# A pair's decays and learning rates, worked out one window earlier

## The chip, the cores and the metric

The kernel runs on one core of a Trainium2 chip. Its time is the device time of one execution in microseconds (us). Before the change, three runs took 1234.54, 1236.76 and 1237.37 us; the median is 1236.76 us. A smaller time is better.

The engines' names are those of the profile: PE multiplies matrices, PEld loads its weights, DVE and ACT work on vectors (ACT also has the tables for tanh, exp and the like), POOL does a few small steps, and SP issues the transfers (DMA) between the large memory and the core's own.

## The reference, cut to what matters

Two layers, each with one mixer. One input projection of the normalised x gives the inputs of two groups of heads; what the change touches is group A, a recurrent mixer that runs over the 256 positions forwards and backwards:

```
h = rms_norm(x, norm_g[l]);  proj = h @ w_in[l]
r, k, v, xw, xa = split(bidir_token_shift(rw_in))
lw = tanh(xw)
for d in (forward, backward):
    decay = exp(-exp(-softplus(-(w0[d] + lw @ decay_up[d])) - 0.5))
    a = sigmoid(a0[d] + xa @ iclr_up[d])          # the learning rates
    kk = k * k_k, normalised within its head
    kd = k * (1 + (a - 1) * k_a)
    S = S * decay - (S kk) (a kk)^T + v kd^T;  y += S r     # position by position
x = x + concat(y_A * silu(g_A), y_B * silu(g_B)) @ w_out[l]
```

Group B is windowed attention. After the second layer comes a last normalisation. decay_up and iclr_up are the low-rank factors (96 rows; with w0 as a further row decay_up has 97) that this document calls du and iu. Group A has 16 heads of 64 channels; the kernel works on pairs of heads, 8 pairs a layer, 128 channels each.

## The kernel before

**The stream of projections.** All large products are cut into output tiles of 128 columns. A tile takes 16 steps, one for each 128 rows of its weights, and a step is three matmuls of 128x256 (L286 to L288), since weights and activations are each split into a high and a low part. The weights come in halves of 8 steps: SP loads `raw` (L208), ACT writes `hi` (L216), DVE writes `lo` (L218). There are three buffers for `raw`, two each for `hi` and `lo`. `Stream.run(n)` emits the next n steps; the function that empties a finished tile (its "evac") is called behind its last step.

**Windows and slots.** A layer starts with two tiles of 16 steps (xw, xa), and then runs in windows of 64 steps, that is four tiles. `window` (L373) cuts a window into 14 slots of four or five steps: slot s begins after step 64*s//14. At the start of each slot it advances the generators that are listed for it, each to its next `yield`, and so puts the mixer's own work between the projections. Window w (0 to 7) projects pair w: k in steps 0 to 15, v to 31, r to 47, the gate gr to 63. From window 8 on the projections are those of the attention. After window 12 the output projection follows with 256 steps, and then the next layer.

**A pair's way through the windows.** Pair p is projected in window p. `scan_p` (L646) prepares it in window p+1, at the slots of STAGE_P. `scan_i` (L724) inverts its chunks in window p+2 and the first two slots after it, and `scan_b` (L874) runs the recurrence in windows p+3 and p+4. So in windows 3 to 7 three or four pairs are in work at once. `scans` (L954) lists the generators with their lag in windows.

`scan_p` has nine stages, at slots 4, 5, 6, 7, 8, 9, 10, 11 and 13:

1. The low-rank products into `pza` (12 matmuls, L636 to L638), ACT's tanh of both (LW for the decay, TH for the learning rate), the square of k (tile `t1`, which the profile calls `t`) and KR.
2. DVE adds 1 to LW and makes two running sums (L672).
3. The head sums `pk` (L642) of the square, ACT's two exponentials PP and IP, DVE's reciprocal KD.
4. to 8. A chain on DVE, which fills MV and BK, and ends with two steps in `km` (tile `lw`).
9. The head sums `pbn` of `km`, and `bv`.

**The low-rank weights.** `ups` (L468) issues the transfers of iu (96 rows, L472) and du (97 rows) into two `g` tiles when the pair's k tile begins. These two buffers are also those of the gate's evacuation (`silu_evac`, L420). `value_evac` (L476) splits them behind the v tile, at step 32: ACT writes iuh and duh (L455), DVE iu and du (L456), each in a single buffer, which the pair before must have read.

**What sets the order.** PE works strictly in the order of the program (`manual_schedule`, L137). For the other engines the framework's planner lays down, when the kernel is built, in which order each engine takes its instructions; among those that it holds to be ready the program's order decides, with a lead for the blocks under `high_priority`. Instructions issued through `PA` (ACT) and `PV` (DVE) keep the program's order among themselves; the splits of iu and du are not among them. At run time each engine takes its list in the given order and waits for whatever is not there yet. SP's queue is such a list too.

Of the kernel before, what the change touches and what calls it, by code (L numbers as in the profile page):

```python
# [15 lines left out]
AF = mybir.ActivationFunctionType  # L16
# [5 lines left out]
T = 256  # L22
# [13 lines left out]
P_NG, P_MU0, P_MU1, P_KK, P_KA, P_RK, P_LG, P_LB, P_A0 = 0, 16, 42, 68, 76, 84, 92, 100, 108  # L36
# [5 lines left out]


SLOTS = 14
STAGE_P = [4, 5, 6, 7, 8, 9, 10, 11, 13]
STAGE_I = (list(range(SLOTS)), [0, 1])
STAGE_B = (list(range(1, 14)), [1, 2, 3, 4])
ATT = [
# [81 lines left out]
def hybrid_trunk_kernel(ctx, tc, xT, wi, wv, wo, par, fing, dup, iup, sink, pos, cst, out):  # L130
# [17 lines left out]
    def wpair(name):  # L148

        return ps_w.tile([128, 2, 512], F32, tag="w", name=name)  # L150

    def wbank(name):
        return wpair(name)[:, 0]

    def st(tag, shape, dt=F32, bufs=1):
        return sp.tile([128, *shape], dt, tag=tag, name=tag, bufs=bufs)
# [76 lines left out]
    PA, PV = InTurn(A), InTurn(V)  # L233
# [167 lines left out]
    def queue_inputs(l):  # L401
        L = layers[l]
        prm = lambda o, j: PR[:, l, o + j : o + j + 1]
        dpm = lambda o, j: DP[:, l, o + j : o + j + 1]

        def inproj(ct, evac, **kw):
            gemm(wi[l, ct], lambda: (L.XH, L.XL), evac, **kw)

        def shift_evac(j, place):
            def evac(pm):  # L410
                dst = place()
                u = st("u", [T], bufs=2)
                V.tensor_tensor(u, pm, L.norm.rb, op=ALU.mult)
                A.activation(dst, u, AF.Identity, scale=dpm(0, j))
                V.scalar_tensor_tensor(dst[:, 1:T], u[:, 0 : T - 1], prm(P_MU0, j), dst[:, 1:T], op0=ALU.mult, op1=ALU.add)
                V.scalar_tensor_tensor(dst[:, 0 : T - 1], u[:, 1:T], prm(P_MU1, j), dst[:, 0 : T - 1], op0=ALU.mult, op1=ALU.add)

            return evac
# [11 lines left out]
        def new(t, name, tag, bufs):  # L430
            def place():
                t[name] = st(tag, [T], bufs=bufs)
                return t[name]

            return place
# [37 lines left out]

            return begin

        def value_evac(p, t):  # L476
            ev = shift_evac(8 + p, new(t, "v", "vg", 8))

            def evac(pm):
                ev(pm)  # L480
                for n, rows in (("iu", RANK), ("du", RANK + 1)):
                    raw = t[n]
                    t[n] = (st(n + "h", [2, 128], F32R), st(n, [2, 128], F32R))
                    split(t[n], raw, rows)

            return evac

        for p, t in enumerate(L.ts):
            inproj(2 + 4 * p, shift_evac(p, new(t, "k", "kr", 4)), begin=ups(p, t))
            inproj(3 + 4 * p, value_evac(p, t))  # L490
            inproj(4 + 4 * p, shift_evac(16 + p, new(t, "r", "kr", 4)))
            inproj(5 + 4 * p, silu_evac(new(t, "gr", "vg", 8)))


# [71 lines left out]
        for n in ("q0", "q1", "q2", "q3", "g0", "q4", "g1", "q5", "g2", "q6", "g3", "q7", "g4", "g5", "g6", "g7"):  # L566
            j = int(n[1])
# [52 lines left out]
    def layer(l):  # L620
# [14 lines left out]
        def low_rank(o, w, x):  # L635
            PE.matmul(o, w[0], x[0], start=True, stop=False)  # L636
            PE.matmul(o, w[0], x[1], start=False, stop=False)
            PE.matmul(o, w[1], x[0], start=False, stop=True)  # L638

        def head_sums(o, x):  # L640
            for r in half:
                PE.matmul(o[r, 0:T], bones[r, r], x[r, 0:T], start=True, stop=True)  # L642

        def scan_p(p, t):  # L646
            K, VV, R, iu, du = t["k"], t["v"], t["r"], t["iu"], t["du"]
            dd = lambda x: x.rearrange("p (d x) -> p d x", d=2)
            two = lambda x: x.unsqueeze(1).to_broadcast([128, 2, T])
            c8 = lambda x: x.rearrange("p (n j) -> p n j", j=64)  # L650

            pza = wpair("pza")
            pz, pa = pza[:, 0], pza[:, 1]
            for d in range(2):
                low_rank(pz[:, d * T : (d + 1) * T], [a[0 : RANK + 1, d, :] for a in du], [a[0 : RANK + 1] for a in L.TW])
            LW = st("lw", [2 * T])
            for d in range(2):
                low_rank(pa[:, d * T : (d + 1) * T], [a[0:RANK, d, :] for a in iu], [a[0:RANK] for a in L.XA])
            PA.activation(LW, pz, AF.Tanh, scale=0.5)
            TH = st("th", [2 * T])  # L660
            for d in range(2):
                PA.activation(TH[:, d * T : (d + 1) * T], pa[:, d * T : (d + 1) * T], AF.Tanh, scale=0.5, bias=dpm(NSH + 16, d * 8 + p))
            sq = st("t1", [T], bufs=3)
            PA.activation(sq, K, AF.Square, scale=prm(P_KK, p))
            KR = st("kkr", [T])
            PA.activation(KR, K, AF.Identity, scale=prm(P_KK, p))
            yield

            PV.tensor_scalar(LW, LW, 1.0, None, op0=ALU.add)
            msk = MSK.rearrange("p c j -> p (c j)")  # L670
            for x in (LW[:, 0:T], LW[:, T : 2 * T][:, ::-1]):
                PV.tensor_tensor_scan(x, msk, x, 0.0, op0=ALU.mult, op1=ALU.add)  # L672
            yield
            pk = wbank("pk")
            head_sums(pk, sq)
            PP = st("pp", [2, NC, 64])
            IP = st("ip", [2, NC, 64])
            PA.activation(PP.rearrange("p d c j -> p (d c j)"), LW, AF.Exp, scale=DECAY_C)
            PA.activation(IP.rearrange("p d c j -> p (d c j)"), LW, AF.Exp, scale=-DECAY_C)
            KD = st("kd", [T])  # L680
            PV.reciprocal(KD, pk[:, 0:T])
            PV.scalar_tensor_tensor(KD, KD, 1e24, KR, op0=ALU.min, op1=ALU.mult)
            yield

            MV = st("mv", [2, NC, 2, 64], bufs=3)
            BK = st("bk", [2, NC, 3, 64])
            km = st("lw", [2 * T])
            kr4 = KR.rearrange("p (c j) -> p c j", j=64)
            PV.scalar_tensor_tensor(MV[:, 0, :, 0, 1:64], PP[:, 0, :, 0:63], -1.0, kr4[:, :, 1:64], op0=ALU.mult, op1=ALU.mult)
            PV.scalar_tensor_tensor(MV[:, 1, :, 0, 0:63], PP[:, 1, :, 1:64], -1.0, kr4[:, :, 0:63], op0=ALU.mult, op1=ALU.mult)  # L690
            PA.activation(MV[:, 0, :, 0, 0:1], kr4[:, :, 0:1], AF.Copy, scale=-1.0)
            PA.activation(MV[:, 1, :, 0, 63:64], kr4[:, :, 63:64], AF.Copy, scale=-1.0)
            PA.activation(km, TH, AF.Identity, scale=dpm(NSH, p), bias=dpm(NSH + 8, p))
            yield
            PV.scalar_tensor_tensor(dd(TH), dd(TH), 1.0, two(KD), op0=ALU.add, op1=ALU.mult)
            BK8 = BK.rearrange("p d c s j -> p (d c) s j")
            IP8 = IP.rearrange("p d c j -> p (d c) j")
            PV.scalar_tensor_tensor(BK8[:, :, 1, :], c8(TH), 0.5, IP8, op0=ALU.mult, op1=ALU.mult)
            yield
            PV.tensor_tensor(dd(km), dd(km), two(K), op=ALU.mult)  # L700
            PV.tensor_tensor(BK8[:, :, 2, :], c8(km), IP8, op=ALU.mult)
            PA.activation(BK8[64:128, :, 0, :], BK8[64:128, :, 2, :], AF.Copy)
            yield
            PV.tensor_tensor(
                MV[:, :, :, 1, :], R.rearrange("p (c j) -> p c j", j=64).unsqueeze(1).to_broadcast([128, 2, NC, 64]), PP, op=ALU.mult
            )
            PC = st("pc", [2, NC], bufs=3)
            PA.activation(PC[:, 0, :], PP[:, 0, :, 63], AF.Copy)
            PA.activation(PC[:, 1, :], PP[:, 1, :, 0], AF.Copy)
            yield  # L710


            PV.tensor_tensor(km[:, 0:T], km[:, 0:T], km[:, T : 2 * T], op=ALU.add)
            PV.scalar_tensor_tensor(km[:, 0:T], km[:, 0:T], prm(P_RK, p), R, op0=ALU.mult, op1=ALU.mult)
            yield
            pb = wbank("pbn")
            head_sums(pb, km)
            bv = st("bv", [T], bufs=3)
            PV.tensor_tensor(bv, pb[:, 0:T], VV, op=ALU.mult)
            t.update(BK=BK, MV=MV, PC=PC, bv=bv)  # L720
            yield
# [232 lines left out]
        def scans(w):  # L954

            gens = []
            for lag, scan, at in ((4, scan_b, STAGE_B[1]), (3, scan_i, STAGE_I[1]), (3, scan_b, STAGE_B[0]), (2, scan_i, STAGE_I[0]), (1, scan_p, STAGE_P)):
                p = w - lag
                if 0 <= p < NP:
                    if (scan, p) not in chains:  # L960
                        chains[scan, p] = scan(p, L.ts[p])
                    gens.append((chains[scan, p], at))
            return gens
# [119 lines left out]
    for a, b in ((0, 2), (2, 4), (4, 8), (8, 12), (12, 16)):  # L1083
        x = X2[:, a:b, :]
# [83 lines left out]
```

## Time and profile before

| | us |
|---|---|
| median of three runs | 1236.76 |
| the profiled execution, its time | 1234.27 |
| its span, first to last instruction | 1232.4 |
| PE busy | 1182.2 |
| DVE busy | 930.7 |
| ACT busy | 743.0 |
| window 0 of layer 0, and of layer 1 | 24.68, 22.52 |
| window 1 of layer 0, and of layer 1 | 35.26, 37.25 |
| window 5 of layer 0 | 42.00 |
| window 8 of layer 0 | 44.87 |

The span counts from the first instruction to the last; some 2 us of the execution's time lie around it. A window is measured from the start of its first step to the start of the next window's. Idle time of PE lengthens the kernel; idle time of another engine does so only where PE waits for it.

How rows are read: in the list of instructions in order of time, a row gives start, duration, engine, line, operation, "out<-in" with the program's tile names, shapes and count; square brackets hold the idle time of the engine just before it, and what ended it. In the view of waits a row gives total, number and longest of the waits. Tiles written through `PA` and `PV` have the helper's line, L231, and are told apart by their names.

### The profile page before, as it was taken

The page shows a single profiled execution, that of the slowest core. Times are in us where ns is not written, and L with a number is a line of the kernel's source. Part 1 is how long each engine was busy: PE and PEld are TensorE (multiplying, and loading weights), DVE is VectorE, ACT ScalarE, POOL GpSimd, SP SyncE. Part 2 cuts the span into 40 slices and gives each one's busy share as a digit, 9 for nine tenths or more (in the row PEclk, how much of TensorE's full clock was granted, in tenths as well). Part 3 has the DMA queues.
Part 4 walks back from the last instruction along what each step waited for, and adds up shares of the span by engine and source line. Part 5 has one row for each costly group of instructions (what it writes and reads, how often), then busy time and mean ns, then how long its engine had stood idle before and what let it go on. Part 6 is the DMA issues. An engine that isn't in the chain of part 4 may idle for free. (4 is left out here: it accounts for less than half of the span.)

```text
span 1232.4 us, 38183 instructions
## 1 busy us (share of the span) xinstructions
PE 1182.2 (96%) x16204; PEld 1096.3 (89%) x16204; DVE 930.7 (76%) x2067; ACT 743.0 (60%) x1838; POOL 19.1 (2%) x23
## 2 busy tenths in 40 slices
PE   6989999999999899999998999999999999999996
PEld 6978998999998889999998889999999888899996
DVE  7878778887876668856676788878887866786654
ACT  6546665766665567655555556675776565665553
POOL 0000000000000000000000000000000000000000
PEclk9999999999999999999999999999999999999998
DMA  7433333323323334467654333333323333445653
GB/s 249 157 136 116 105 117 109 105 96 114 119 89 99 117 112 144 140 214 240 209 182 147 124 128 93 106 111 111 105 94 106 124 102 127 131 130 178 211 192 121
DMA packets 60411, 166.72 MB, mean 135 GB/s; under 512 B 7728, under 2 KB 22736, under 8 KB 60240
## 3 DMA queue, kind: packets, MB, share of 16 engines
q1 hardware_dynamic: 60240, 164.27, 41.0%
q8 instruction: 127, 2.08, 0.7%
q14 instruction: 44, 0.36, 0.1%
HBM read 157.43 MB, written 4.19 MB: 131 GB/s over the span
## 5 line engine op out<-in xcount | busy, mean ns | idle before, releaser
L286 PE MATMUL pm<-XH,hi 128*128 128x256 f32 x1664 | 498.8, 300 | 9.4 <-ACT XH L179 5.9
L288 PE MATMUL pm<-XH,lo 128*128 128x256 f32 x1664 | 471.5, 283 | 4.8 <-DVE lo L218 4.6
L287 PE MATMUL pm<-XL,hi 128*128 128x256 f32 x1664 | 471.8, 284 | 0.1
L216 ACT ACTIVATE hi<-raw 128x512 fp32r<-128x512 f32 x560 | 328.1, 625 | 238.0 <-PE pm L287 147.9
L218 DVE TENSOR_TENSOR lo<-raw,hi 128x512 fp32r<-128x512 f32 x560 | 368.4, 687 | 96.7 <-ACT hi L216 89.2
L286 PEld LDWEIGHTS pm<-XH,hi 128*128 128x128 f32 x1664 | 317.3, 191 | 34.9 <-issue 13.0
L288 PEld LDWEIGHTS pm<-XH,lo 128*128 128x128 f32 x1664 | 318.3, 191 | 6.5 <-DVE lo L218 6.4
L287 PEld LDWEIGHTS pm<-XL,hi 128*128 128x128 f32 x1664 | 318.3, 191 | 0.9 <-DVE XL L180 0.9
L286 PE MATMUL pm<-MH,hi 128*128 128x256 f32 x512 | 144.1, 281 | 1.2 <-ACT hi L216 1.2
L288 PE MATMUL pm<-MH,lo 128*128 128x256 f32 x512 | 143.9, 281 | 0.4 <-DVE lo L218 0.4
L287 PE MATMUL pm<-ML,hi 128*128 128x256 f32 x512 | 143.8, 281 | 0.0
L286 PEld LDWEIGHTS pm<-MH,hi 128*128 128x128 f32 x512 | 96.6, 189 | 2.2 <-ACT hi L216 1.4
L288 PEld LDWEIGHTS pm<-MH,lo 128*128 128x128 f32 x512 | 96.6, 189 | 0.6 <-DVE lo L218 0.6
L287 PEld LDWEIGHTS pm<-ML,hi 128*128 128x128 f32 x512 | 96.6, 189 | 0.0
L908 ACT ACTIVATE suv<-pcc 64x128 f32<-64x128 f32 x128 | 34.2, 267 | 18.1 <-PE pq L835 11.8
L837 ACT ACTIVATE QF<-pq 128x256 f16<-128x256 f32 x80 | 30.8, 385 | 19.8 <-PE pq L835 19.0
L993 ACT ACTIVATE mv<-mv,mx 128x257 f32<-128x257 f32 x64 | 32.0, 503 | 17.5 <-DVE mx L990 17.3
L740 DVE TENSOR_TENSOR ge<-pg,C 128x1024 f32<-128x1024 f32 x32 | 39.1, 1221 | 3.2 <-PE pg L734 3.1
L844 DVE CAST_PREDICATED tv<-LV,pd 128x256 f16<-128x256 uint8 x80 | 34.4, 430 | 7.7 <-PE pd L843 6.9
L892 ACT ACTIVATE rh<-pcc 128x128 f32<-128x128 f32 x64 | 17.5, 273 | 35.4 <-PE pcc L890 35.0
L734 PE MATMUL pg<-mv,bk 64*128 64x128 f32 x512 | 37.2, 285 | 0.0
L845 DVE CAST_PREDICATED tt<-LV,pd 128x256 f16<-128x256 uint8 x80 | 34.1, 426 | 0.0
(239 smaller groups left out, 1845.8 us busy)
## 6 DMA issues: line engine op xcount, KB each, us to landing
raw<-wi SPq DMA_DIRECT2D x207, 512.0 KB, 3.3
raw<-wo SPq DMA_DIRECT2D x64, 512.0 KB, 4.3
raw<-wv SPq DMA_DIRECT2D x8, 512.0 KB, 3.3
rrot<-u SPq DMA_DIRECT2D x80, 32.0 KB, 2.0
vg<-xT SPq DMA_DIRECT2D x16, 128.0 KB, 4.6
xd<-vg SPq DMA_DIRECT2D x16, 128.0 KB, 2.4
vg<-xd SPq DMA_DIRECT2D x16, 128.0 KB, 3.3
g<-dup SPq DMA_DIRECT2D x16, 97.0 KB
```

The source lines that it names most:

```text
L216: A.activation(hi[:, q], raw[:, q], AF.Copy)
L218: V.tensor_tensor(lo[:, q], raw[:, q], hi[:, q].bitcast(F32), op=ALU.subtract)
L286: PE.matmul(pm, wh, rh[:, kk, :], start=(kk == 0), stop=False)
L287: PE.matmul(pm, wh, rl[:, kk, :], start=False, stop=False)
L288: PE.matmul(pm, wl, rh[:, kk, :], start=False, stop=(kk == 15))
L734: PE.matmul(pg[:, h, c * 128 : (c + 1) * 128], BK[half[h], d, c, 1 - h : 3 - h, :].rearrange("p s j -> p (s j)"), MV[half[h], d, c].rearra ...
L740: V.tensor_tensor(GEd(d), pg.rearrange("p h (c x) -> p h c x", c=NC), gm[d].unsqueeze(1).unsqueeze(1).to_broadcast([128, 2, NC, 128]), op= ...
L837: A.activation(t_sub(QF), flat4(pq[:, :, 0:128]), AF.Copy)
L844: V.copy_predicated(t_sub(TC), t_mask, flat4(pd[:, :, 0:128]))
L845: V.copy_predicated(v_sub(TT), v_mask, flat4(pd[:, 0, 128:384].rearrange("p (d x) -> p d x", d=2)))
L908: A.activation(here(h), pc[half[h], 1], AF.Copy)
L993: A.activation(Sc[:, h, q, 0:257], Sc[:, h, q, 0:257], AF.Exp, scale=0.125, bias=mx[:, q : q + 1], accum_out=den[:, q : q + 1])
```

## The change

`scan_p` is cut in two. A new generator `scan_d` holds the low-rank products, the two tanh, the addition and the two running sums. It has lag 0: it runs in the pair's own window, at slots 12 and 13, behind the r tile. What is left of `scan_p` has nine stages again, now at slots 3 to 11: the square and KR alone in the first, the two exponentials alone in the second, `pk` and KD in the third, and the rest as before, each one or two slots earlier. The split of iu and du goes from behind the v tile (step 32) to behind the r tile (step 48).

```
-STAGE_P = [4, 5, 6, 7, 8, 9, 10, 11, 13]
+STAGE_D = [12, 13]
+STAGE_P = [3, 4, 5, 6, 7, 8, 9, 10, 11]
...
-        def value_evac(p, t):
-            ev = shift_evac(8 + p, new(t, "v", "vg", 8))
+        def receptance_evac(p, t):
+            ev = shift_evac(16 + p, new(t, "r", "kr", 4))
...
-            inproj(3 + 4 * p, value_evac(p, t))
-            inproj(4 + 4 * p, shift_evac(16 + p, new(t, "r", "kr", 4)))
+            inproj(3 + 4 * p, shift_evac(8 + p, new(t, "v", "vg", 8)))
+            inproj(4 + 4 * p, receptance_evac(p, t))
...
+        def scan_d(p, t):
+
+            iu, du = t["iu"], t["du"]
             pza = wpair("pza")
             pz, pa = pza[:, 0], pza[:, 1]
...
+            t.update(LW=LW, TH=TH)
+            yield
+
+            PV.tensor_scalar(LW, LW, 1.0, None, op0=ALU.add)
+            msk = MSK.rearrange("p c j -> p (c j)")
+            for x in (LW[:, 0:T], LW[:, T : 2 * T][:, ::-1]):
+                PV.tensor_tensor_scan(x, msk, x, 0.0, op0=ALU.mult, op1=ALU.add)
+            yield
+
+        def scan_p(p, t):
+            K, VV, R, LW, TH = t["k"], t["v"], t["r"], t["LW"], t["TH"]
...
             KR = st("kkr", [T])
             PA.activation(KR, K, AF.Identity, scale=prm(P_KK, p))
             yield
...
             PA.activation(PP.rearrange("p d c j -> p (d c j)"), LW, AF.Exp, scale=DECAY_C)
             PA.activation(IP.rearrange("p d c j -> p (d c j)"), LW, AF.Exp, scale=-DECAY_C)
+            yield
+            pk = wbank("pk")
+            head_sums(pk, sq)
             KD = st("kd", [T])
...
-(1, scan_p, STAGE_P)):
+(1, scan_p, STAGE_P), (0, scan_d, STAGE_D)):
```

No instruction is added or left out: the same ones are emitted in another order.

More of the change, by code (lines that the diff above doesn't have):

```diff
@@ L642, in head_sums @@
                 PE.matmul(o[r, 0:T], bones[r, r], x[r, 0:T], start=True, stop=True)
[L646 to L650, printed above, removed]
+        def scan_d(p, t):
+            iu, du = t["iu"], t["du"]
             pza = wpair("pza")
@@ L655, in scan_p @@
                 low_rank(pz[:, d * T : (d + 1) * T], [a[0 : RANK + 1, d, :] for a in du], [a[0 : RANK + 1] for a in L.TW])
-            LW = st("lw", [2 * T])
             for d in range(2):
                 low_rank(pa[:, d * T : (d + 1) * T], [a[0:RANK, d, :] for a in iu], [a[0:RANK] for a in L.XA])
+            LW = st("lw", [2 * T])
             PA.activation(LW, pz, AF.Tanh, scale=0.5)
@@ L662, in scan_p @@
                 PA.activation(TH[:, d * T : (d + 1) * T], pa[:, d * T : (d + 1) * T], AF.Tanh, scale=0.5, bias=dpm(NSH + 16, d * 8 + p))
[L663 to L666, printed above, removed]
+            t.update(LW=LW, TH=TH)
             yield
@@ L673, in scan_p @@
             yield
-            pk = wbank("pk")
-            head_sums(pk, sq)
+        def scan_p(p, t):
+            K, VV, R, LW, TH = t["k"], t["v"], t["r"], t["LW"], t["TH"]
+            dd = lambda x: x.rearrange("p (d x) -> p d x", d=2)
+            two = lambda x: x.unsqueeze(1).to_broadcast([128, 2, T])
+            c8 = lambda x: x.rearrange("p (n j) -> p n j", j=64)
+            sq = st("t1", [T], bufs=3)
+            PA.activation(sq, K, AF.Square, scale=prm(P_KK, p))
+            KR = st("kkr", [T])
+            PA.activation(KR, K, AF.Identity, scale=prm(P_KK, p))
+            yield
             PP = st("pp", [2, NC, 64])
@@ L956, in scans @@
             gens = []
-            for lag, scan, at in ((4, scan_b, STAGE_B[1]), (3, scan_i, STAGE_I[1]), (3, scan_b, STAGE_B[0]), (2, scan_i, STAGE_I[0]), (1, scan_p, STAGE_P)):
+            for lag, scan, at in ((4, scan_b, STAGE_B[1]), (3, scan_i, STAGE_I[1]), (3, scan_b, STAGE_B[0]), (2, scan_i, STAGE_I[0]), (1, scan_p, STAGE_P), (0, scan_d, STAGE_D)):
                 p = w - lag
```

## The prediction, made before the result was known

> **What bounds the kernel now.** I read the page first, then the busy time of each engine by window (a window is the stretch of 64 projection steps that the text above describes; its bounds are the starts of its first step and of the next window's).
>
> ```profile
> span 1232.4 us, 38183 instructions
> PE 1182.2 (96%) x16204; PEld 1096.3 (89%) x16204; DVE 930.7 (76%) x2067; ACT 743.0 (60%) x1838; POOL 19.1 (2%) x23
> ...
> 53.96:89.22 35.26, 28.86 (x231) 27.25 (x229) 26.61 (x52) 18.92 (x39) 0.00 (x0) 0.95 0.46 154
> 89.22:125.99 36.77, 35.71 (x568) 32.20 (x566) 31.82 (x63) 23.10 (x52) 0.00 (x0) 1.00 0.37 122
> 209.55:251.55 42.00, 42.00 (x757) 38.13 (x755) 35.42 (x75) 27.84 (x74) 1.01 (x1) 1.00 0.33 107
> 655.49:692.74 37.25, 30.55 (x231) 28.65 (x229) 24.68 (x46) 17.53 (x38) 0.00 (x0) 0.91 0.40 133
> ```
>
> The window rows give length, then busy time of PE, PEld, DVE, ACT, POOL, then granted clock, DMA share and GB/s. Window 5 of layer 0 (209.55 to 251.55) stands for windows 3 to 7 of both layers: PE is busy for all 42.00 us, so nothing that is only moved about there can gain. Window 1 of each layer (first and last row) is the opposite: PE is idle for 6.4 and 6.7 us, and its clock falls below 1. The view of waits says on whom PE waits, and the timeline where:
>
> ```profile
> PE pbn L642 <- DVE lw L231: 5.6, 2, 2.8
> PE pk L642 <- ACT t L231: 5.4, 2, 2.9
> ...
> 69.07 0.65 PE L642 MATMUL pk<-t,C 64*64 64x256 f32 x4 [2.92 <-ACT t L231]
> 85.59 0.65 PE L642 MATMUL pbn<-lw,C 64*64 64x256 f32 x4 [2.77 <-DVE lw L231]
> ```
>
> Both waits come once a layer, in window 1. The first is a wait for ACT's square of k (L664), and ACT was late for a reason that decides this case:
>
> ```profile
> 61.82 0.49 ACT L414 ACTIVATE kr<-u,DP 128x256 f32<-128x256 f32 x1
> 66.70 0.42 ACT L455 ACTIVATE duh<-g 97x256 fp32r<-97x256 f32 x1 [4.38 <-DMA g<-dup]
> 67.33 0.57 ACT L231 ACTIVATE lw<-pza 128x512 f32<-128x512 f32 x1
> ...
> 59.07 0.30 SPq L472 DMA_DIRECT2D g<-dup  x1
> ```
>
> ACT stood for 4.38 us at the split of the next pair's decay weights (duh), because their transfer, issued at 59.07, landed at about 66.70, 7.6 us later; the work of the current pair (lw, th, t) was queued behind it.
>
> **The change, part by part.** (1) *Window 1.* The low-rank matmuls (pza), the two tanh and the scan leave it for window 0, so the square of k no longer has them, nor the split that pushed in ahead of them, in front of it. I take the whole pk wait as gone: 5.4 us for both layers. After each of these waits the clock fell:
>
> ```profile
> 69.07:74.50 5.43, 5.43 (x32) 5.05 (x33) 5.34 (x9) 4.87 (x11) 0.00 (x0) 0.69 0.09 20
> 85.59:91.00 5.41, 5.41 (x49) 4.64 (x51) 3.02 (x6) 1.46 (x3) 0.00 (x0) 1.00 0.17 68
> ```
>
> 5.43 us at a clock of 0.69 lose 5.43 x 0.31 = 1.7 us, 3.4 us for two layers. Against this, pk to pbn shrinks from slots 6 to 13 (steps 27 to 59) to slots 5 to 11 (steps 22 to 50), 28 steps for 32, while DVE's chain between them stays as long; 4 steps at 0.36 us (rows at 217.21 and 217.57 below) add 1.4 us to the pbn wait, 2.8 for both. And ACT's wait for the transfer stays in window 1, now in front of the weight splits (L216). What that costs, the output projection shows, where the same split met only weight splits:
>
> ```profile
> 539.94 0.30 SPq L472 DMA_DIRECT2D g<-dup  x1
> ...
> 538.52 1.16 ACT L216 ACTIVATE hi<-raw 128x512 fp32r<-128x512 f32 x2 [1.65 <-PE pm L287]
> ...
> 541.41 1.15 ACT L216 ACTIVATE hi<-raw 128x512 fp32r<-128x512 f32 x2 [1.03 <-issue]
> 542.47 0.40 ACT L455 ACTIVATE iuh<-g 96x256 fp32r<-96x256 f32 x1
> 547.38 0.42 ACT L455 ACTIVATE duh<-g 97x256 fp32r<-97x256 f32 x1 [4.50 <-DMA g<-dup]
> ...
> 548.36 0.39 PE L286 MATMUL pm<-MH,hi 128*128 128x256 f32 x1 [1.22 <-ACT hi L216]
> 549.24 0.38 PE L288 MATMUL pm<-MH,lo 128*128 128x256 f32 x1 [0.37 <-DVE lo L218]
> ```
>
> 4.50 us of ACT became 1.22 + 0.37 = 1.6 us of PE; 3.2 for both layers. Window 1 in all: -5.4 - 3.4 + 2.8 + 3.2 = -2.8 us, between -8.8 (both gains alone) and +2.
>
> (2) *Windows 3 to 7: the split loses its cover.* Before, a pair's iu and du cannot be split until the pza matmuls of the pair before have read the single buffers, in slot 4. That holds the split back to +13 us of a window, when the transfer has landed. After the change those matmuls have run in the window before, in slot 12, and the split is free as soon as its data is believed to be there. That it now stands at step 48 of the program and not 32 does not hold it back: the rows above at 542.47 and 547.38 are layer 1's first split, worked while PE was in layer 0's output projection (operand MH), far ahead of its place. The planner fills idle ACT time with whatever it takes to be ready. In window 5:
>
> ```profile
> 210.30 0.42 SPq L472 DMA_DIRECT2D g<-iup  x1
> 210.78 0.30 SPq L472 DMA_DIRECT2D g<-dup  x1
> ...
> 212.83 0.28 ACT L892 ACTIVATE rh<-pcc 128x128 f32<-128x128 f32 x1
> 214.96 1.15 ACT L216 ACTIVATE hi<-raw 128x512 fp32r<-128x512 f32 x2 [1.85 <-issue]
> 216.02 0.54 ACT L908 ACTIVATE suv<-pcc 64x128 f32<-64x128 f32 x2
> 216.58 1.28 ACT L231 ACTIVATE AB<-ge 64x512 f16<-64x512 f32 x2
> ...
> 222.61 0.42 ACT L455 ACTIVATE duh<-g 97x256 fp32r<-97x256 f32 x1
> ```
>
> ACT idles for 1.85 us before 214.96; then it is solidly busy. When does the planner believe du landed? In the output projection it had put the split ahead of the next weight split, due at 541.41 + 2.89 = 544.3 by the spacing of the two above, so it believed in a landing within 4.4 us of the issue at 539.94. In window 1 it had put it ahead of lw, whose matmuls stand 9 steps of 0.36 us before pk, where PE arrived at 69.07 - 2.92 = 66.15: about 62.9, within 3.8 us of 59.07. Both are estimates, read from the order. 3.8 us after 210.78 is 214.6, inside the idle gap: I expect the split there. The real landing is 210.78 + 7.6 = 218.4. ACT then takes the weight split at 218.4 + 0.42 = 218.8 for 214.96, 3.9 us late, and suv and AB behind it equally late. PE uses them here:
>
> ```profile
> 217.21 0.28 PE L286 MATMUL pm<-XH,hi 128*128 128x256 f32 x1
> 217.57 0.28 PE L286 MATMUL pm<-XH,hi 128*128 128x256 f32 x1
> ...
> 218.00 0.45 PE L913 MATMUL pcc<-suv,bt 128*64 128x64 f32 x8
> ...
> 218.62 0.33 PE L825 MATMUL pq<-tv,AB 64*64 64x32 f16 x10
> ```
>
> AB ended at 216.58 + 1.28 = 217.86 and was needed at 218.62: 0.76 us of slack. So PE loses 3.9 - 0.76 = 3.1 us. PE was full, so all of it lengthens the window: ten windows, 31 us. Is 7.6 us right for all of them? The view of waits and that of the tile:
>
> ```profile
> ACT duh L455 <- DMA g<-dup: 17.4, 4, 4.6
> ...
> DMA to landing us min/median/max: 2.9/3.5/4.8
> ```
>
> Four times ACT waited for dup, and each time it had been issued at least 7.4 us before (547.38 - 539.94); the landings that the second row gives are those of iup. Had the other twelve landed in 3.5 us, the split would find its data at 214.3, and this term would be 0. [...] I take 3.1; the ends are 0 and 5.0, the longest of the four waits (4.6) with the split's 0.42 and no slack.
>
> (3) *The clock after these stalls.* The rows above show one of 2.92 us followed by a lower clock and one of 2.77 not. A stall of 3.1 lies by both, so I count 1.7 us after every second one: 8.5 us, between 0 and 17. [...]
>
> (4) *Slot 13.* The scan now comes beside the predicated copies on which the next slot's pf waits.
>
> ```profile
> 68.67 1.27 DVE L231 TENSOR_TENSOR_SCAN lw<-MSK,lw 128x256 f32<-128x256 f16 x2
> ...
> 249.12 0.42 DVE L845 CAST_PREDICATED tt<-LV,pd 128x256 f16<-128x256 uint8 x1
> ...
> 249.94 0.30 PE L851 MATMUL pf<-tv,NEYE 64*64 64x256 f16 x4
> ```
>
> The copy ends 0.4 us before pf. If the scan goes first, and since pbn's 0.65 us leaves that slot, which brings pf nearer, up to 1.27 us are lost in each of the 12 windows that have both: 15 us at most. Now the same scan stands in slot 5, beside the same kind of copies, in windows without PE idle time; I take 0.
>
> (5) *At nothing.* The 12 pza matmuls go from window 8 to window 0 on balance; PE is full in both, and they cost the same. In layer 0's window 0 the two tanh may fall between the sines of the set-up and bring two more table loads:
>
> ```profile
> 49.57 1.28 ACT L358 ACT_TABLE_LOAD   x1
> ```
>
> 2.6 us of an engine that holds up nothing there; 0, at most 2.6. The raw iu and du tiles are held to step 48 instead of 32, but the gate's evacuation, which needs them next, comes at step 64; no transfer is issued later. Window 2: ACT has another gap and may miss the wait; 0, at most 5 us each. The later place of pk, the square and the exponentials change no PE work in full windows.
>
> Sum: -2.8 + 31 + 8.5 = +36.7 us on 1234.27 us of the profiled execution (span 1232.4): 1271. That execution lies 2.5 us below the median of 1236.76.
>
> **The rivals.** *It gains* (faster): the planner expects du later than the gap's end, 4.2 us after its issue; then the solid ACT work, earlier in the program, goes first, until about 222, and the data is there. That decides it, and my bounds of 3.8 and 4.4 lie astride. Then only window 1 counts, without ACT's wait: -8.8 + 2.8 = -6 us, 1228. *The scan crowds slot 13* (slower by another way), with no wait for du: 15 - 6 = +9 us, 1243; it decides from the point where the copy ends 0.4 us later. For it speaks that small margin, against it slot 5 of now. *It does not do what it says*: ACT and DVE already run ahead of their place, the full windows stay full, and what pk gives pbn takes back: 1233 to 1236.
>
> **How the numbers follow.** Chances: forecast 0.62, gain 0.20, slot 13 0.10, no change 0.08. About 0.2% (2.5 us) is what a measurement can tell from no change. Slower is 0.62 + 0.10 = 0.72, same 0.08, faster 0.20. The forecast's own range is 1254 (ten times 2.9, for a landing after 7.4 us, no clock loss, window 1 at its best) to 1298 (ten times 5.0, a clock loss after each). To leave out no more than two in ten, the range reaches down to the gain: 1228 to 1298.
>
> **What would show it.** Right: in windows 3 to 7 the view of waits has some ten new waits of ACT's duh for g<-dup of about 4 us, PE waits at L913 and L825, windows of 45 to 47 us for 42.0, no pk wait, a larger pbn wait. Wrong: windows 3 to 7 still at 42.0, and duh behind suv on ACT with no wait; or, for slot 13, PE waits at L851.

## The result, and the profile after

The changed kernel takes 1297.54 us (median of four runs, 1296.23 to 1299.41) against 1236.79 for the kernel before (four runs): a ratio of 1.0496, with a 95% interval of 1.0477 to 1.0514. The change makes the kernel slower by 60.8 us. The profiled execution took 1296.23 us, 62.0 more than that of before.

The page of the kernel after, its span and its first part:

```profile
span 1294.5 us, 38194 instructions
...
PE 1200.4 (93%) x16204; PEld 1110.3 (86%) x16204; DVE 929.9 (72%) x2067; ACT 749.1 (58%) x1840; POOL 19.2 (1%) x23
```

All engines have the same work, but for two more instructions of ACT: the table loads that the prediction's (5) had allowed for. PE is "busy" for 18 us more, and for a PE with the same instructions that means a lower clock (its mean is 0.972, for 0.990 before); the other 44 us are idle time of PE. Busy time by window of the kernel after: windows 1, 2, 5 and 8 of layer 0, and window 1 of layer 1.

```profile
53.85:87.60 33.75, 29.71 (x231) 27.61 (x229) 26.13 (x51) 19.77 (x41) 0.00 (x0) 0.90 0.43 145
87.60:130.91 43.31, 37.76 (x568) 33.91 (x566) 30.76 (x61) 22.63 (x50) 0.00 (x0) 0.96 0.36 113
225.21:272.89 47.68, 43.55 (x757) 39.41 (x755) 35.44 (x75) 28.27 (x73) 1.01 (x1) 0.96 0.30 95
367.67:410.02 42.35, 40.74 (x745) 36.79 (x743) 32.95 (x69) 26.80 (x71) 1.10 (x1) 1.00 0.31 100
685.75:718.94 33.19, 29.64 (x231) 27.73 (x229) 24.43 (x47) 17.52 (x37) 0.00 (x0) 0.90 0.41 134
```

Window 5 went from 42.00 to 47.68 us, with 4.1 us of PE idle and a clock of 0.96 where there had been neither. Summed over both layers, after minus before:

| windows | us |
|---|---|
| 0 | +1.6 |
| 1 | -5.6 |
| 2 | +13.1 |
| 3 to 7 | +55.0 |
| 8 | -4.1 |
| 9 to 12 | +2.4 |

The view of waits of the kernel after says on whom ACT and PE waited:

```profile
ACT duh L456 <- DMA g<-dup: 64.3, 15, 5.2
ACT iuh L456 <- DMA g<-iup: 34.6, 14, 5.2
...
PE pcc L911 <- ACT rh L900: 36.5, 11, 3.9
...
PE pq L833 <- ACT AB L232: 8.1, 4, 3.6
PE pbn L643 <- DVE lw L232: 7.4, 4, 3.4
...
PE pg L742 <- DVE ge L748: 4.4, 12, 0.7
```

(Lines stand one lower than in the kernel before, or more: rh is L900 for L892, the split L456 for L455.) ACT's wait for dup has grown from 17.4 us in 4 to 64.3 in 15, and it has a companion for iup. No wait for pk is left. Window 5 on ACT, and where PE felt it:

```profile
225.65 0.58 ACT L866 ACTIVATE q<-pf 128x512 f16<-128x512 f32 x1
228.25 0.42 ACT L456 ACTIVATE iuh<-g 96x256 fp32r<-96x256 f32 x1 [2.02 <-DMA g<-iup]
233.59 0.42 ACT L456 ACTIVATE duh<-g 97x256 fp32r<-97x256 f32 x1 [4.93 <-DMA g<-dup]
233.92 0.55 ACT L950 ACTIVATE t<-py,PR 128x256 f32<-128x256 f32 x1
234.37 0.59 ACT L878 ACTIVATE vf<-pn 128x512 f32<-128x512 f32 x1
234.84 0.28 ACT L900 ACTIVATE rh<-pcc 128x128 f32<-128x128 f32 x1
```

```profile
226.63 0.30 SPq L473 DMA_DIRECT2D g<-dup  x1
```

```profile
235.17 0.38 PE L911 MATMUL pcc<-rh,vf 64*64 64x64 f32 x5 [3.83 <-ACT rh L900]
```

Both splits stand in ACT's list right behind q, in front of t, vf and rh. SP issues du at 226.63; it has landed 7.0 us later, at 233.59. ACT does nothing in between except iuh, and PE stands 3.83 us for rh, the third in ACT's list behind the late du.

### The profile page after: what moved, and what is told of

The parts are those of the page before. It is cut to its first block, busy times and chain, and to the rows that moved or that the text cites. A ratio compares the mean times of both kernels' runs of the same rounds, so it can differ in the third digit from the quotient of the medians.

```text
span 1294.5 us, 38194 instructions
## 1 busy us (share of the span) xinstructions
PE 1200.4 (93%) x16204; PEld 1110.3 (86%) x16204; DVE 929.9 (72%) x2067; ACT 749.1 (58%) x1840; POOL 19.2 (1%) x23
## 5 line engine op out<-in xcount | busy, mean ns | idle before, releaser
L287 PE MATMUL pm<-XH,hi 128*128 128x256 f32 x1664 | 503.9, 303 | 10.0 <-ACT XH L180 6.5
L287 PEld LDWEIGHTS pm<-XH,hi 128*128 128x128 f32 x1664 | 321.9, 193 | 36.4 <-issue 13.8
L289 PEld LDWEIGHTS pm<-XH,lo 128*128 128x128 f32 x1664 | 322.5, 194 | 6.8 <-DVE lo L219 6.7
L288 PEld LDWEIGHTS pm<-XL,hi 128*128 128x128 f32 x1664 | 323.1, 194 | 0.7 <-DVE XL L181 0.7
L911 PE MATMUL pcc<-rh,vf 64*64 64x64 f32 x512 | 26.7, 223 | 36.5 <-ACT rh L900 36.5
L911 PEld LDWEIGHTS pcc<-rh,vf 64*64 64x64 f32 x512 | 20.5, 136 | 39.4 <-ACT rh L900 38.8
L457 DVE TENSOR_TENSOR du<-g,duh 97x256 fp32r<-97x256 f32 x16 | 6.8, 424 | 58.5 <-ACT duh L456 58.5
L456 ACT ACTIVATE duh<-g 97x256 fp32r<-97x256 f32 x16 | 6.7, 416 | 64.3 <-DMA g<-dup 64.3
L1001 ACT ACTIVATE mv<-mv,mx 128x257 f32<-128x257 f32 x64 | 31.9, 503 | 17.6 <-DVE mx L998 17.4
```

Of the source, the lines that this page charges most:

```text
L287: PE.matmul(pm, wh, rh[:, kk, :], start=(kk == 0), stop=False)
L288: PE.matmul(pm, wh, rl[:, kk, :], start=False, stop=False)
L289: PE.matmul(pm, wl, rh[:, kk, :], start=False, stop=(kk == 15))
L456: A.activation(hi, x[0:rows], AF.Copy)
L457: V.tensor_tensor(lo, x[0:rows], hi.bitcast(F32), op=ALU.subtract)
L911: PE.matmul(pc[half[h], 1, d, :], t["VF"][half[h], d, cs(ci[d])], RH[half[h], d, :], start=True, stop=True)
```

## The experiments

The theory: since the matmuls that read the single buffers of iu and du now run a window earlier, nothing holds the split back any more; the planner puts it where it believes du to be there, du's transfer of 97 rows is later than that, and ACT stands with the work of the other pairs queued behind it. The rival: the stages themselves, at slots 12, 13 and 3 to 11, crowd DVE and ACT beside the other three pairs, and the wait for du is only where this shows. All times of a batch stand against runs of the kernel before on the same chip (1234.38, 1234.72 and 1233.46 us).

**Splitting in turn.** ACT's half of the split is issued through `PA`, so that it keeps its place in the program's order, behind the r tile. All stages stay moved.

```
-        def split(hl, x, rows):
+        def split(hl, x, rows, on=A):
...
-            A.activation(hi, x[0:rows], AF.Copy)
+            on.activation(hi, x[0:rows], AF.Copy)
...
-                    split(t[n], raw, rows)
+                    split(t[n], raw, rows, PA)
```

> The changed kernel; only ACT's half of the split of iu and du is put among the instructions that keep the program's order on ACT, so it can no longer be taken ahead of its place. Theory (ACT stands for du's transfer, with the recurrence's copies queued behind it): no wait of duh for g<-dup in windows 1 to 7, windows 3 to 7 back from 47.5 to 42 to 42.6 us, time 1226 to 1237 us. Rival 1 (the new slots themselves cost: DVE's scans beside the predicated copies, a shorter stretch from pk to pbn): time stays above 1270 us, since the slots are those of the changed kernel.

1236.96 us, ratio 1.0027 (1.0014 to 1.0040). The view of waits has no wait of ACT for dup or iup at all. Window 5 of this kernel by the view of windows, and the waits of PE for DVE that have come or come oftener (the kernel before has the second 4 times, 3.5 us in all, and the other two not at all):

```profile
211.56:254.79 43.23, 42.19 (x756) 38.15 (x754) 35.23 (x75) 28.36 (x73) 1.01 (x1) 1.00 0.33 105
```

```profile
PE pg L742 <- DVE ge L748: 4.6, 12, 0.8
PE pq L843 <- DVE tv L852: 3.7, 10, 1.0
PE pq L843 <- DVE tt L853: 2.8, 8, 0.3
```

Of the 5.7 us that window 5 had lost, 4.5 come back with the place of two instructions in a list, and the clock is back at 1.00. The rest, 1.2 us, is the rival's: waits of PE for DVE, three of 0.3 us in this window. So the rival is right about a fifth of the loss in these windows.

**Raw tiles of their own.** iu and du are loaded into two tiles that lie idle until the attention, instead of those of the gate's evacuation, so their loads can be issued nearly a window earlier.

```
-                    t[n] = st("g", [2, 128], bufs=2)
+                    t[n] = st("KA" if n == "iu" else "VA", [2, 128])
```

> The changed kernel; iu and du are loaded into two tiles of their own (those that the attention uses later), not into the gate's two, so their transfers no longer wait for the gate of the pair before and are issued up to a window earlier. Theory: the data is there when ACT comes to the split, no wait for g<-dup in windows 2 to 7, windows 3 to 7 at 42 to 42.6 us, time 1226 to 1237 us. Rival 1 (slots): above 1270 us. Rival 2 (the split's own work on ACT and DVE falls in a bad place whether its data is there or not): above 1250 us.

1235.68 us, ratio 1.0007 (0.9994 to 1.0020): the same time as before the change, with another cure of the same wait. Window 5, and what is left of ACT's wait for dup, all of it outside windows 2 to 7:

```profile
212.93:255.58 42.65, 42.11 (x757) 38.17 (x755) 35.08 (x75) 28.02 (x74) 1.01 (x1) 1.00 0.32 105
```

```profile
ACT duh L456 <- DMA VA<-dup: 11.6, 3, 4.2
```

**The reverse, in the kernel before.** No stage is moved. Only the high parts of iu and du get a second buffer (the same idle tiles, for every other pair), so that the split no longer waits for the pair before.

```
-                    t[n] = (st(n + "h", [2, 128], F32R), st(n, [2, 128], F32R))
+                    hi = n + "h" if p % 2 == 0 else ("KA" if n == "iu" else "VA")
+                    t[n] = (st(hi, [2, 128], F32R), st(n, [2, 128], F32R))
```

> The kernel before, with its stages and slots untouched; only iuh and duh of every second pair go into other tiles, so the split no longer has to wait for the low-rank products of the pair before. Theory: the split is taken early as in the changed kernel, ACT waits 3 to 5 us for g<-dup in windows 2 to 7, windows 3 to 7 take 45 to 48 us, time 1275 to 1305 us, without any stage having moved. Rival 1 (slots): 1233 to 1240 us.

1295.25 us, ratio 1.0492 (1.0465 to 1.0518): as much as the change loses, with none of its stages moved. The view of waits, and window 5 on ACT (the tile of du's high part is called VA in this pair):

```profile
ACT VA L455 <- DMA g<-dup: 32.3, 8, 4.9
ACT duh L455 <- DMA g<-dup: 32.0, 8, 4.6
PE pcc L914 <- ACT suv L909: 28.0, 11, 3.6
...
PE pq L826 <- ACT AB L231: 10.5, 11, 3.4
```

```profile
230.81 0.42 ACT L455 ACTIVATE KA<-g 96x256 fp32r<-96x256 f32 x1 [1.11 <-DMA g<-iup]
235.92 0.42 ACT L455 ACTIVATE VA<-g 97x256 fp32r<-97x256 f32 x1 [4.05 <-DMA g<-dup]
236.25 1.13 ACT L216 ACTIVATE hi<-raw 128x512 fp32r<-128x512 f32 x2
237.28 0.54 ACT L909 ACTIVATE suv<-pcc 64x128 f32<-64x128 f32 x2
```

32.3 + 32.0 = 64.3 us of waits for dup, as in the kernel after. Here the split stands exactly where the prediction had put it, in front of hi, suv and AB, and PE waits for suv and AB. This is the experiment that decides: the lost cover alone is enough for a loss of this size. That the two totals are so close is partly chance: windows 2 to 7 take 62 us more here and 68 in the kernel after, which gets 5.6 back in window 1 where this one gets 1.2.

**The place in the program.** The kernel after, with the split back behind the v tile at step 32.

```
-        def receptance_evac(p, t):
-            ev = shift_evac(16 + p, new(t, "r", "kr", 4))
+        def value_evac(p, t):
+            ev = shift_evac(8 + p, new(t, "v", "vg", 8))
...
-            inproj(3 + 4 * p, shift_evac(8 + p, new(t, "v", "vg", 8)))
-            inproj(4 + 4 * p, receptance_evac(p, t))
+            inproj(3 + 4 * p, value_evac(p, t))
+            inproj(4 + 4 * p, shift_evac(16 + p, new(t, "r", "kr", 4)))
```

> The changed kernel with the split of iu and du back behind the v tile (step 32 of the program) instead of behind the r tile (step 48). Theory: its place in the program does not count as long as the planner takes it when it believes the data there: 1294 to 1301 us, the same waits. Rival 3 (the later place is what costs): near 1237 us.

1297.67 us, ratio 1.0506 (1.0476 to 1.0536). Step 48 or 32 makes no difference that this measurement can tell: the planner is free to place these two instructions, and here their place in the program held nothing back.

**Du in two loads.** In the kernel before, iu's 96 rows landed 2.9 to 4.8 us after their issue, and the last packet of du's 97 ended 6.5 to 7.9 us after it. If the number of rows is what makes dup late, 96 rows and one row should land as early as iu does. In the kernel after, with `rows` 96 for iu (one load as ever) and 97 for du:

```
-                    SY.dma_start(out=t[n][0:rows], in_=src[l, :, :, p * 128 : (p + 1) * 128].rearrange("d r c -> r d c"))
+                    for a, b in ((0, RANK), (RANK, rows)):
+                        if a < b:
+                            SY.dma_start(out=t[n][a:b], in_=src[l, :, a:b, p * 128 : (p + 1) * 128].rearrange("d r c -> r d c"))
```

> The changed kernel; du's 97 rows are loaded as 96 and 1, so one load a pair more is issued. Theory (the late landing of the 97-row load is what ACT stands for): the 96 rows land like iu's, 3 to 4 us after their issue, ACT takes duh some 3.5 us earlier, PE's wait for the recurrence's copies falls from 3.8 to under 1 us in windows 3 to 7, the half clock behind it goes too, time 1234 to 1244 us. Rival 4 (the split is merely taken too early, any transfer would be late by as much): above 1270 us.

1234.22 us, ratio 1.0000 (0.9988 to 1.0011). Window 5 on ACT and on SP's queue:

```profile
211.85 0.42 ACT L456 ACTIVATE iuh<-g 96x256 fp32r<-96x256 f32 x1 [2.07 <-DMA g<-iup]
212.17 0.55 ACT L952 ACTIVATE t<-py,PR 128x256 f32<-128x256 f32 x1
212.62 0.40 ACT L456 ACTIVATE duh<-g 97x256 fp32r<-97x256 f32 x1
```

```profile
210.18 1.06 SPq L475 DMA_DIRECT2D g<-dup  x2
```

Issued at 210.18, du is taken at 212.62 without a wait, 2.4 us later; as one load it had taken 7.0. Where the time goes in one load, the packets in the trace of the kernel after show: in window 5 the 192 packets of iu start between 227.23 and 227.87 us, and the 194 of du follow one by one, some 24 ns apart, until 232.85. The wait for iup stays (37.0 us in 14), and in window 5 it costs PE nothing (the 0.5 us that PE is idle there are waits for DVE); window 2 of layer 0, where the wait for iup is over 5 us long, still takes 39.40 us for 36.77.

**The same in the kernel before.**

> The kernel before with du loaded as 96 rows and 1. Theory: only window 1 had the wait; pk's wait (5.4 us over both layers) and the half clock behind it shrink, pbn's stays, time 1226 to 1234 us. Rival: the chain on DVE that ends in pbn takes all of it back, 1233 to 1237 us.

1223.34 us, ratio 0.9906 (0.9894 to 0.9919): faster than both kernels, and below the 1226 to 1234 that I had expected. Windows 1 of both layers and window 5, and the one wait that is left of the two in window 1:

```profile
51.14:84.23 33.09, 28.96 (x230) 27.13 (x229) 26.55 (x52) 19.12 (x40) 0.00 (x0) 0.95 0.51 164
204.88:246.88 42.00, 42.00 (x756) 38.12 (x754) 35.41 (x75) 27.80 (x74) 1.01 (x1) 1.00 0.33 106
647.70:680.88 33.18, 29.83 (x230) 27.82 (x228) 25.09 (x47) 17.68 (x38) 0.00 (x0) 0.90 0.48 149
```

```profile
PE pbn L644 <- DVE lw L231: 6.0, 2, 3.2
```

Window 1 is as short here (33.09 and 33.18 us) as in the changed kernel (33.75 and 33.19), with no stage moved. The wait for pk, the only thing that the change could take away, had come from dup. Of the 11.1 us between the two profiled spans window 1 gives 6.2 over both layers. Another 2.1 lie in layer 0's output projection, where the same wait had stood, and some 3 in layer 0 up to the end of window 0, where ACT had stood 4.6 us for the first du; the expectation had counted window 1 alone.

**Raw tiles of their own, in the kernel before.**

> The kernel before with iu and du loaded into two tiles of their own, which frees their transfers from the gate of the pair before. Theory: as with the two loads, no wait for g<-dup in window 1, 1226 to 1234 us. Rival: pbn takes it back, 1233 to 1237 us.

1226.99 us, ratio 0.9944 (0.9929 to 0.9958). It gains as well, but less: layer 0's window 0 grew from 24.68 to 26.78 us. The set-up work stands in another order there (ACT's table load of L358 at 44.77 us for 49.57), but that this is the cause is not shown.

**Du's load issued ahead of iu's.** If ACT stands until du has landed, an issue 0.4 us earlier should shorten the stand. In the kernel after:

```
-                for n, src, rows in (("iu", iup, RANK), ("du", dup, RANK + 1)):
+                for n, src, rows in (("du", dup, RANK + 1), ("iu", iup, RANK)):
```

> The changed kernel with du's load issued ahead of iu's. Theory: du lands about 0.4 to 0.5 us earlier, each of the waits in windows 2 to 7 is shorter by that, 12 x 0.45 = 5 us, 1290 to 1295 us; if the half clock needs stalls of 3.4 us or more it also goes in most of these windows (another 1.7 us each), 1270 to 1280 us. Rival 4: 1297 us, unchanged.

1297.97 us, ratio 1.0509 (1.0496 to 1.0523), a miss: I had expected a gain of a few us. The view of waits and one window:

```profile
PE pcc L911 <- ACT rh L900: 32.6, 11, 3.7
```

```profile
860.57:908.51 47.94, 44.40 (x756) 40.19 (x754) 35.32 (x75) 28.11 (x73) 1.01 (x1) 0.93 0.29 94
```

PE's waits for rh did shrink, by 36.5 - 32.6 = 3.9 us, and windows 2 to 7 together take 2.6 us less than in the kernel after. But two things took it back. In the window shown the granted clock is 0.93 and PE is busy for 44.40 us, for 0.96 and 43.55 us in window 5 of the kernel after. And window 1 takes 1.8 us more over both layers: in layer 1 ACT now stands 6.8 us for du in front of the weight splits, and PE 2.4 us for the first of them. The limit of 3.4 us that the expectation considers for the half clock is shown by no run: in the kernel after a stall of 2.99 us was followed by half clock, in the kernel before one of 2.78 us was and one of 2.77 was not (the last section).

**Both cures together,** to see what the stages cost by themselves. The kernel after, with two loads and the split in turn:

> The changed kernel with both cures, du loaded as 96 rows and 1 and ACT's half of the split kept in the program's order, so neither du nor iu can hold ACT up early. What is left against the kernel before with the two loads (1223.3 us) is what the new slots themselves cost. Theory now (the wait was nearly all of the loss, the slots cost little but not nothing: 0.6 to 1.2 us in each of windows 3 to 7): 1230 to 1236 us. Rival (the stages in their new slots are free once both waits are out): 1221 to 1226 us.

1236.89 us, ratio 1.0025 (1.0011 to 1.0039), a little above what was expected; windows 4 to 7 take 43.23 us again. And the kernel before, with two loads and raw tiles of their own:

> The kernel before with du loaded as 96 rows and 1, and with tiles of their own for both loads. Theory: once du lands like iu, its earlier issue has nothing left to take: 1221 to 1227 us, as with the two loads alone (1223.3) or slightly more for the changed order of the set-up in window 0, which cost some 3 us with tiles of their own. Rival: iu's transfer still held window 1 up, and 1 to 3 us more are gained, below 1222 us.

1223.14 us, ratio 0.9909 (0.9888 to 0.9929): the second cure adds nothing to the first. So with dup out of the way the kernel before takes 1223 us and the changed one 1234 to 1237. The stages in their new slots cost 11 to 14 us (1234.22 less 1223.34, and 1236.89 less 1223.14), and don't gain; by the profiles, some 12 of the 14 lie in windows 3 to 7.

## Why the prediction was wrong in size, and right in kind

The direction and the mechanism were as forecast: ACT's new waits for dup in windows 3 to 7, windows of 47 us for 42.0, no pk wait. The sum was +36.7; the profiled execution shows +62.0. Two steps failed. Window 2 was put at nothing and took 13.1 us. The clock was to fall after every second stall of windows 3 to 7, for 8.5 us, and fell after each, for 15. Term by term:

| step | forecast, us | measured, us |
|---|---|---|
| (1) window 1 | -2.8 | -5.6 |
| (2) windows 3 to 7, PE's stalls | +31 | +36 |
| (3) the clock after these stalls | +8.5 | +15 |
| (4) slot 13; here PE's other idle time in windows 3 to 7 | 0 | +4 |
| (5) window 2 | 0 | +13.1 |
| (5) windows 0 and 8 to 12 | 0 | -0.1 |

The rows (2) to (4) share out the 55.0 us of windows 3 to 7. PE is idle for 40 us there, where it had not been idle at all: 36 for rh, and 4 elsewhere, mostly for ge. The other 15 us are PE's busy time, which rose by some 1.5 us a window, as from 42.00 to 43.55 in window 5.

(1) The pk wait went, as forecast, and the gain is all idle time: PE's 6.4 and 6.7 us in window 1 became 33.75 - 29.71 = 4.0 and 33.19 - 29.64 = 3.6. The two terms set against it were too large: the wait for pbn in window 1 rose from 5.6 to 6.9 us over both layers, by 1.3 for 2.8 (the other two of the four pbn waits, 0.3 us each, lie in window 2), and ACT's stand in window 1 is short, 1.51 us, and costs PE nothing for the 3.2 that I took from the output projection. But the clock's 3.4 us didn't come back: the longer pbn wait now brings a stretch of 6.83 us at half clock in both layers. Before, layer 0 had one stretch of 3.41 us, behind pk's wait, and layer 1 had two, behind a wait for lo at 673.66 and behind pbn's; the prediction had put the first of these two down to pk. The granted clock of window 1 is 0.90 in both layers, for 0.95 and 0.91.

(2) The step that I had to choose, whether the planner takes du for landed 3.8 us behind its issue, came out on the forecast's side. The place was wrong: it put iuh and duh right behind q, so ACT also waits 2 us for iup, and rh is what comes late, not suv and AB. PE's loss, 3.0 to 3.9 us a window, is near the 3.1 forecast. That every dup is late, four waits had to show for sixteen; now 15 waits show it. The trace of the kernel before had it already: the last packet of each of the sixteen ends 6.5 to 7.9 us after du's issue, also where no wait showed it. The two loads show that the single load made it late: in window 5, 97 rows at once take 7.0 us, as 96 and 1 at most 2.4.

(3) This is the step that failed most in kind: "after every second one". All ten stalls in windows 3 to 7, 2.99 to 3.91 us long, were followed by 3.41 us at half clock. The 1.7 us that was counted for each is near what it cost, 1.5. The prediction's two stalls, 2.92 us with a lower clock behind it and 2.77 without, differ less in length than in how they lie on the grid of the last section, where the rows are.

(4) The scan did not crowd pf in slot 13. What the moved stages delay is other work of DVE: PE waits for ge (L748) at pg, and, once ACT's stand is cured, for tv and tt at pq.

(5) "Window 2: ACT has another gap and may miss the wait; 0, at most 5 us each" was the largest mistake: 13.1 us, 6.5 a window. Window 2 of layer 0, on ACT and on PE:

```profile
92.86 0.42 ACT L456 ACTIVATE iuh<-g 96x256 fp32r<-96x256 f32 x1 [4.86 <-DMA g<-iup]
97.49 0.42 ACT L456 ACTIVATE duh<-g 97x256 fp32r<-97x256 f32 x1 [4.21 <-DMA g<-dup]
97.81 1.26 ACT L232 ACTIVATE AB<-ge 64x512 f16<-64x512 f32 x2
```

```profile
98.47 0.20 PE L833 MATMUL pq<-tv,AB 64*64 64x32 f16 x1 [3.61 <-ACT AB L232]
```

It did not miss the wait: ACT stands 9 us for the two splits, AB is behind them, and PE stands 3.61 us for AB and 0.5 more right after, in both layers. That is 4.1 us, inside the bound. The slow stretch behind it I had counted for no window but 3 to 7; PE's busy time rose by 37.76 - 35.71 = 2.0 us. The split lost its cover here as in the windows behind, so the term should have had the value of the others. Windows 0 and 8 show the low-rank products' way from the one to the other, +1.6 and -4.1, with windows 9 to 12 nearly nothing on balance, as forecast. That PE was full in both did not hold: in window 8 of layer 0 it had been idle for 2.7 us, and is for 1.6.

Of the rivals, the gain needed a planner that expects du later; crowding is real, but costs some 0.3 us a time, and not at pf. None of them held that the gain in window 1 is to be had without the change. The prediction had read from ACT's row in window 1 that the pk wait was dup's doing, and did not conclude that the load, not the stages, was the thing to change. That the measured time lies at the upper end of the range says little for its parts: that end was worked out with 5.0 us a window for the stalls, which took 3.6, and with nothing for window 2.

## What to carry to other kernels

When a change takes a dependence away, look for the instructions that it had held back by accident: the planner can move them up, as it did here, to a place where their data is not there yet, and a late transfer then stops everything queued behind them on that engine (in window 5, 4.93 us of ACT became 3.83 us of PE). A wait on an engine that isn't the bottleneck is cheap only as long as nothing that the bottleneck needs stands behind it (ACT's 1.51 us in window 1 cost PE nothing); so ask for each such wait what is next in that engine's list, in every window where it occurs. And mend the late transfer first: loading 97 rows as 96 and 1 gave 0.94% by itself, which moving the stages could not.

## What the runs showed of the hardware

**Slow stretches began on a grid of 3.41 us.** In the kernel after, the five slow stretches of windows 3 to 7 of layer 0 begin at 140.32, 188.11, 235.90, 283.68 and 331.47 us, 47.79 us or 14 times 3.413 apart; all 18 that begin between 40 and 1200 us in the two kernels' profiles, before and after, lie a whole number of 3.413 us from one another within their profile (to 0.01 us). On this grid the idle share of one period sorts the cases, where the length of a stall does not. Periods of the kernel before, round its two stalls in window 1 of layer 0 (length, PE busy, and the granted clock as the third number from the end):

```profile
67.10:70.51 3.41, 1.44 (x11) 1.06 (x12) 3.33 (x7) 2.85 (x8) 0.00 (x0) 1.00 0.03 11
70.51:73.92 3.41, 3.41 (x18) 3.41 (x18) 3.32 (x6) 3.41 (x9) 0.00 (x0) 0.50 0.00 0
80.75:84.16 3.41, 2.06 (x18) 1.85 (x16) 3.31 (x8) 2.43 (x6) 0.00 (x0) 1.00 0.56 190
84.16:87.57 3.41, 1.98 (x16) 1.63 (x17) 1.67 (x4) 0.00 (x0) 0.00 (x0) 1.00 0.58 207
87.57:90.99 3.42, 3.42 (x36) 3.04 (x36) 2.59 (x5) 1.46 (x3) 0.00 (x0) 1.00 0.00 0
```

The stall of 2.92 us leaves a period with 1.97 of 3.41 us idle (58%), and the next one runs at half clock. The stall of 2.77 us is cut by the grid into 1.35 (40%) and 1.43 us (42%), and nothing follows. In layer 1 a stall of 2.78 us (684.83 to 687.61) lies almost whole in one period, which is idle for 2.70 us (79%), and the next one runs at half clock. In window 5 of the kernel after:

```profile
232.49:235.90 3.41, 0.73 (x27) 0.66 (x28) 1.83 (x5) 2.31 (x6) 0.00 (x0) 1.00 0.07 25
235.90:239.31 3.41, 3.41 (x24) 3.18 (x24) 2.20 (x4) 3.29 (x8) 0.00 (x0) 0.50 0.15 29
```

Worked out in this way for the profiles of these two kernels between 40 and 1200 us, all 16 periods in which PE was idle for 58% or more were followed by one at half clock; of the 630 with at most 36% and a full clock, none was; of the 13 between, with 37% to 52%, four were. By this spacing a stall of 3.8 us, wherever it lies, leaves some period idle for at least 1.9 us (56%), and one of 2.8 us leaves two with 1.4 us (41%) if its middle falls on a boundary. What decides between 36% and 58%, and why a slow stretch sometimes lasts two periods (6.83 us from 75.47 on, after window 1's stall), stays open.

**One load of 97 rows landed later than one of 96 and one of 1.** In window 5 du was taken 7.0 us after its issue as one load, and 2.4 us after the first issue as two, issued by SP in both cases, at the price of one more issue. Over all sixteen pairs of the kernel before, the last packet of the one load ends 6.5 to 7.9 us after the issue, and ACT waits 17.4 us for dup, in 4 waits; with two loads the view of waits has no wait for dup of 1.0 us or more.
